# Another order of block products, background work tied behind weight splits, and two projections moved up in the third group

## The chip, the cores and the metric

The kernel runs on one core of a Trainium2 chip. The metric is the device time of one execution in microseconds (us). The kernel before took 1521.1 us, the median of three runs (1520.48 to 1521.79).

The engines of the core have these names in the profile: TensorE is PE (its weight loads are PEld), VectorE is DVE, ScalarE is ACT, GpSimd is POOL. SP issues most of the transfers (DMAs). Each engine has a queue of its own and runs it in order.

## The reference

Two layers of a mixer run on 256 tokens of width 2048, in float32, and a last RMS normalization follows:

```
u  = rms_norm(x, norm_g);  p = u @ w_in
qk, v, o, z_a, ig, fg, xb, z_b = split(p)
qk = silu(causal_dwconv(qk));  q, k = split(qk)
h  = mlstm_chunkwise(q, k, v, ig + i_bias, log_sigmoid(fg + f_bias))
h  = head_norm(h * sigmoid(o)) * head_norm_g;   y_a = h * silu(z_a)
xc = causal_dwconv(xb) + b
r, i = sigmoid(xc @ w_a + b_a), sigmoid(xc @ w_x + b_x)         # per head
log_a = -8 * r * softplus(-lam)
y_b = scan(h = a*h + xc*i*sqrt(1 - a^2)) * silu(z_b)
x  = x + concat(y_a, y_b) @ w_out
```

There are 8 mLSTM heads and 8 RG-LRU heads. The product with `w_in` (2048 by 12304) and the one with `w_out` (4096 by 2048) are most of the arithmetic.

## The kernel before

**Splits.** All products have to be as good as float32. TensorE's fast format keeps fewer bits, so each operand is split: a high part H (a cast on ScalarE, L344 of `prepare`, tile `wH`) and the low part L = value - H (a subtraction on VectorE, line L345, in the profile L189, the helper `tt_`; tile `wL`). A product is then three matmuls: H by H, H by L and L by H. The weights come from memory in units of 128 x 2048, which are worked off in two halves of 128 x 1024. `mm_a` makes 12 matmuls of 512 columns for each half.

**Order of the work.** `_sequence` lists the units of both layers. A layer has four groups of heads. A group consists of the projections o, qk, v, xb, z and zb (4 units, 8 halves each), the gate products (1 unit) and the output chunks of the group before (4 chunks of 2 units). The main loop (L1336) walks over the halves. At step n it first prepares the splits up to half n + 3 (`AHEAD = 3`; there are four buffers for H and four for L), then emits the matmuls of half n and what follows a finished accumulation (the `_post` functions, which evacuate PSUM).

**Background.** What follows a projection (convolutions, scores, the recurrence, the gate vector of the mLSTM) is written as generators in the queue `bg`. After each plain half, `pump` (L245) lets the generators run from the front until a budget is spent: 1.05 if at most two of them count, else 2.6. A generator yields the cost of what it has just emitted, or "wait" to be passed over, or None to end this turn of the pump. If something is needed now, `require` (L265) runs generators without a budget until it is there. The emitted program is then put into each engine's queue by a planner, which goes by its own estimate of when an instruction can run, and among those that can by the order of emission. `order(a, b)` (L237) makes the planner put a after b. It costs no instruction.

**Changes of layout.** `to_channels` turns a result from token order to channel order: ScalarE copies it to `tok`, VectorE transposes blocks of it to `blk`, four DMAs on SP's queue write it to memory as `moved`, and one DMA on Pool's queue reads it back as `fr`. q/k, xb and zb go through it, and so do z times the normalized heads, and x at the border of the layers. `joined` (L509) then copies `fr` to `ch` for the convolution.

**Block products.** The z projection of the third group and the o projection of the fourth (`PAIR`) have no place of their own in the order. Together they are a product of x, cut into 2 by 2 blocks (token half by half of the 2048 inputs), with weights cut into 2 by 2 blocks (input half by projection), and `block_halves` makes them in seven block products where eight would be the plain way. Products 5, 6, 7 and 3 need sums of blocks of x: `block_sums` makes S1 to S4 on VectorE (`sum_t`, `sums`) with a cast on ScalarE, in two buffers. Products 5, 6, 7 and 4 need sums of blocks of weights: `weight_sums` makes them in memory (`wd`, in the profile `w_d`) with DMAs, the first term as a copy on SP's queue, the others as accumulating DMAs on Pool's queue, one every four turns of the pump. Each product is four block halves of 6 matmuls; its result collects in one PSUM bank (`ps_b`) and is copied or added into one of four slots of `res`. The 28 block halves of a layer are spread evenly over a span of plain halves, except the eight halves that begin with a gate unit. The span of layer 0 begins with qk of the second group, that of layer 1 with v of the first (L1314); both end ahead of the third group's gates, where `z_post` takes the z result from `res`.

**The gate vector.** `first_gen` (L1146) of a layer makes the row scales, then `gates_gen` (tile `scs`: sums, a logarithm by a polynomial in `log1p_exp_half`, two scans), in layer 0 `lam_gen` (the same polynomial for lam, tile `lams`), then `gates_tr`, which puts the result at `at`, and it starts `block_sums`.

Of the kernel before, what the change touches and what calls it, by code (L numbers as in the profile page):

```python
# [16 lines left out]
P = 128  # L17
# [15 lines left out]
BLOCKS_AHEAD = 5  # L33

# [5 lines left out]
def _sequence():  # L40
# [54 lines left out]
def tile_trunk(ctx, tc, x, xt, par, gw, gb, ws, final_g, out):  # L95
    nc = tc.nc
    V, S, G, PE = nc.vector, nc.scalar, nc.gpsimd, nc.tensor
# [101 lines left out]
    def log1p_exp_half(x_, tl, behind=None):  # L199
# [5 lines left out]
        S.activation(out=z, in_=z, func=AF.Exp)  # L205
        d = tl("d")
        ts_(d, z, 2.0, ALU.add)
        V.reciprocal(out=d, in_=d)
        s = tl("s")
# [14 lines left out]
    def lam_gen():  # L224
        lams = work.tile([P, 4, DEPTH, 16], F32, tag="tok", name="lams")

        def tl_lam(nm):
            return lams[:, "zdsn".index(nm)]

        ql = log1p_exp_half(lam, tl_lam, st["split_end"])  # L230
# [314 lines left out]
    def gates_gen(l):  # L545
# [27 lines left out]
        G.memset(sT, 0.0)  # L573
        stt(sT[0:8, :], gi, gbs[:, l, 0:1], Fc, ALU.add, ALU.subtract)
# [10 lines left out]
        yield 3  # L585
# [231 lines left out]
    def gate_post(l, g):  # L817
        def gen():
            xc, _ = st["xc", l, g]
# [167 lines left out]
    def block_sums(l):  # L987
# [22 lines left out]
        def s2(two, a, k, ks):  # L1010
            order(stt(two[a], sums[0].bitcast(F32)[:, a, ks], -1.0, part(0, 0, a, k), ALU.mult, ALU.subtract), st["wL"])
# [4 lines left out]
        def s4(two, a, k, ks):  # L1016
            order(stt(two[a], sums[1].bitcast(F32)[:, a, ks], -1.0, part(0, 1, a, k), ALU.mult, ALU.subtract), st["wL"])
# [5 lines left out]
        while ("done", l, 5) not in st:  # L1023
            yield "wait"
        yield from made(0, "S3", s3)
        while ("done", l, 6) not in st:
# [8 lines left out]
    def weight_sums():  # L1035

        def moved(l, to, start, r, c):
            for j in range(2):
                for h in range(2):
                    cs = slice(1024 * h, 1024 * h + 1024)  # L1040
# [8 lines left out]
        for l in range(DEPTH):  # L1049
            yield from moved(l, 0, True, 0, 0)  # L1050
            yield from moved(l, 0, False, 0, 1)
            yield from moved(l, 1, True, 1, 1)
            yield from moved(l, 1, False, 0, 1)
            while ("loaded", l, 5) not in st:
                yield "wait"
            yield from moved(l, 0, False, 1, 1)
            while ("loaded", l, 6) not in st:
                yield "wait"
            yield from moved(l, 0, False, 1, 0)

    def block_halves(l):
# [19 lines left out]
        def end6():  # L1081
            add(1, 1, box["b"])
            add(3, 3, slot(1))

        def end7():
            add(2, 3, box["b"])
            add(1, 1, box["b"])

        def end4():
            add(1, 1, box["b"])  # L1090
            g1 = PAIR[1][1]

            def gen():
                while ("lru", l, g1 - 1) not in st:
                    yield "wait"
                o_post(l, g1, (slot(3), slot(2)), "neg")
# [22 lines left out]
        for no, A, need, end, W in (  # L1119
            (5, summed(0), "S1", lambda: copied(3), 0),  # L1120
            (1, plain(0, 0), None, lambda: copied(1), (0, 0)),
            (2, plain(0, 1), None, lambda: add(0, 1, box["b"]), (1, 0)),
            (6, summed(1), "S2", end6, 0),
            (7, summed(0), "S3", end7, 1),
            (3, summed(1), "S4", lambda: add(3, 3, box["b"]), (1, 1)),
            (4, plain(1, 1), None, end4, 0),
        ):
            for kp in range(4):
# [3 lines left out]
                if kp == 3:  # L1132
                    hf["loaded"] = ("loaded", l, no)
# [323 lines left out]
```

## Time and profile before

| | |
|---|---|
| median of three runs | 1521.1 us |
| the profiled execution | 1520.76 us |
| its span, first to last instruction | 1519.0 us |
| mean granted TensorE clock | 0.989 |
| PE busy | 1483.0 us, 98% |
| DVE busy | 1137.4 us, 75% |
| ACT busy | 969.9 us, 64% |
| POOL busy | 108.3 us, 7% |

Times inside a profile count from the start of the span. A busy share is the share of the span in which an engine had an instruction under way. The granted clock says at what part of its full speed TensorE was allowed to run. A row of groups has line, engine, operation, output<-inputs, shapes, count, then busy us, mean ns of one, and the idle time of the engine ahead of them with what ended it. A row of waits has the total, the number of waits and the longest.

### The profile page before, as it was taken

What the parts mean: (1) busy time and instruction counts of PE and PEld (TensorE: products, weight loads), DVE (VectorE), ACT (ScalarE), POOL (GpSimd) and SP (SyncE); (2) the same over time, 40 slices, a digit from 0 to 9 for tenths busy, and PEclk for the clock granted to TensorE, in tenths of its full rate; (3) what the DMA queues carried; (4) which work ended last, traced back from release to release, by engine and by line L of the source; (5) the groups of instructions that cost most, each with busy time, mean ns of one, the idle gap of its engine ahead of it and who ended that gap; (6) DMA issues with size and microseconds to landing.
All of it is one profiled execution on the core that took longest, in us unless ns stands there. A gap on an engine that the chain in (4) does not pass through costs nothing.

```text
span 1519.0 us, 18863 instructions
## 1 busy us (share of the span) xinstructions
PE 1483.0 (98%) x6782; PEld 1229.6 (81%) x6782; DVE 1137.4 (75%) x1616; ACT 969.9 (64%) x1259; POOL 108.3 (7%) x186
## 2 busy tenths in 40 slices
PE   9999999999999999999997899999999999999997
PEld 7878778888888878888885788888888888788886
DVE  5879977678757875778858897875886578766785
ACT  7656766567556775658664568754675567665675
POOL 0020011001000010000001100000000000000002
PEclk9999999999999999999999899999999999999999
DMA  9779798888889997876875696768976677678783
GB/s 348 277 244 280 277 281 246 274 276 276 284 264 311 281 269 251 251 258 218 286 269 153 195 279 230 256 203 257 282 260 233 218 239 224 213 243 267 238 277 111
DMA packets 104046, 383.44 MB, mean 252 GB/s; under 512 B 11392, under 2 KB 31888, under 8 KB 84496
## 3 DMA queue, kind: packets, MB, share of 16 engines
q1 hardware_dynamic: 87536, 327.41, 62.2%
q0 software_dynamic: 13952, 50.35, 15.2%
q10 hardware_dynamic: 2464, 4.47, 0.8%
q8 instruction: 53, 0.87, 0.2%
q14 instruction: 41, 0.34, 0.1%
HBM read 344.95 MB, written 62.41 MB: 268 GB/s over the span
## 4 chain that ended last, share of the span: by engine, by line
PE 85%; DVE 7%; DMA 4%; issue 3%; ACT 1%; POOL 0%; SPq 0%; DVEq 0%; POOLq 0%; ACTq 0%
PE acc L368 71%; PE ps_gt L807 3%; DVE wL L189 2%; PE ps_b L1108 2%; PE ps_b L1109 2%; PE ps_b L1107 2%; PE acc L381 1%; DMA raw<-in_ws_dram 1%; DMA moved<-blk 1%; DVE scs L189 1%; DMA w_d<-in_ws_dram 1%; PE acc L1202 1%; PE acc L1203 1%; PE acc L1201 1%; DMA fr<-moved 1%
## 5 line engine op out<-in xcount | busy, mean ns | idle before, releaser
L368 PE MATMUL acc<-wH,x_s 128*128 128x512 f32 x2752 | 865.4, 391 | 4.1 <-ACT wH L344 4.0
L189 DVE TENSOR_TENSOR wL<-raw,wH 128x1024 fp32r<-128x1024 f32 (+1 forms) x500 | 597.3, 1203 | 248.8 <-ACT wH L344 246.7
L344 ACT CAST wH<-raw 128x1024 fp32r<-128x1024 f32 (+1 forms) x500 | 513.9, 1037 | 339.3 <-PE acc L368 279.0
L368 PEld LDWEIGHTS acc<-wH,x_s 128*128 128x128 f32 x2752 | 519.4, 189 | 114.2 <-ACT wH L344 6.8
L368 PE MATMUL acc<-wL,x_s 128*128 128x512 f32 x1376 | 538.4, 392 | 21.1 <-DVE wL L189 21.1
L368 PEld LDWEIGHTS acc<-wL,x_s 128*128 128x128 f32 x1376 | 260.0, 189 | 78.2 <-DVE wL L189 24.9
L368 PE MATMUL acc<-wH,yaH 128*128 128x512 f32 x224 | 87.5, 390 | 0.0
L368 PE MATMUL acc<-wH,ybL 128*128 128x512 f32 x224 | 87.3, 390 | 0.0
L368 PE MATMUL acc<-wL,yaH 128*128 128x512 f32 x224 | 87.3, 390 | 0.0
L368 PE MATMUL acc<-wH,yaL 128*128 128x512 f32 x224 | 87.3, 390 | 0.0
L368 PE MATMUL acc<-wL,ybH 128*128 128x512 f32 x224 | 87.2, 389 | 0.0
L368 PE MATMUL acc<-wH,ybH 128*128 128x512 f32 x224 | 87.2, 389 | 0.0
L189 DVE TENSOR_TENSOR wL<-rawb,wH 128x1024 fp32r<-128x1024 f32 x56 | 68.4, 1222 | 23.7 <-ACT wH L344 21.5
L344 ACT CAST wH<-rawb 128x1024 fp32r<-128x1024 f32 x56 | 58.9, 1051 | 35.8 <-PE acc L368 25.8
L489 POOL DMA_DIRECT2D fr<-moved x34 | 19.3, 566 | 514.7 <-DMA moved<-blk 380.1
L485 DVE STREAM_TRANSPOSE blk<-tok 128x1024 f32<-128x1024 f32 x33 | 40.9, 1240 | 17.9 <-ACT tok L475 17.9
L368 PEld LDWEIGHTS acc<-wH,ybL 128*128 128x128 f32 x224 | 42.1, 188 | 9.0 <-DVE ybL L189 0.3
L368 PEld LDWEIGHTS acc<-wH,yaL 128*128 128x128 f32 x224 | 42.0, 188 | 8.7
L368 PEld LDWEIGHTS acc<-wL,ybH 128*128 128x128 f32 x224 | 42.0, 188 | 8.6
L368 PEld LDWEIGHTS acc<-wH,ybH 128*128 128x128 f32 x224 | 42.1, 188 | 8.6
L368 PEld LDWEIGHTS acc<-wH,yaH 128*128 128x128 f32 x224 | 42.1, 188 | 8.5
L368 PEld LDWEIGHTS acc<-wL,yaH 128*128 128x128 f32 x224 | 42.1, 188 | 8.2
(234 smaller groups left out, 1657.9 us busy)
## 6 DMA issues: line engine op xcount, KB each, us to landing
raw<-in_ws_dram SPq DMA_DIRECT2D x152, 1024.0 KB, 5.9
raw<-in_ws_dram SPq DMA_DIRECT2D x190, 512.0 KB, 6.2
fr<-moved POOLq DMA_DIRECT2D x34, 512.0 KB, 5.2
moved<-blk SPq DMA_DIRECT2D x132, 128.0 KB, 2.8
w_d<-in_ws_dram POOLq DMA_DIRECT2D x32, 512.0 KB, 12.8
rawb<-w_d SPq DMA_DIRECT2D x32, 512.0 KB, 6.8
rawb<-in_ws_dram SPq DMA_DIRECT2D x24, 512.0 KB, 5.4
x_d<-stage POOLq DMA_DIRECT2D x24, 512.0 KB, 7.2
```

Source lines behind the costliest of these rows:

```text
L189: return V.tensor_tensor(out=o, in0=a, in1=b, op=op)
L344: st["wH"] = S.copy(out=H[:, o], in_=r[:, o])
L368: st["mm"] = PE.matmul(o, a_[:, kt, P * t : P * t + P], W[:, k], start=b, stop=z)
L381: PE.matmul(ps[:, ct, T * part : 2 * T], W[:, k, P * ct : P * ct + P], moving, start=first and k == 0 and part == 0, stop=last and k == 3 ...
L485: V.transpose(out=blk.rearrange("p m n -> p (m n)"), in_=tok.rearrange("p m c t j -> p (m c t j)"))
L489: i0 = back.dma_start(out=fr.rearrange("p a c t i -> p a (c t i)"), in_=moved)
L807: PE.matmul(o, W[:, ib, jl], xs[:, ib, a, :], start=j == 0 and i == 0 and W is Hv and a == 0, stop=i == 1 and W is Lv, skip_group_check=True)
L1107: PE.matmul(box["b"], aH, Hv[:, k], start=kp == 0 and k == 0, stop=False)
L1108: PE.matmul(box["b"], aH, Lv[:, k], start=False, stop=False)
L1109: PE.matmul(box["b"], aL, Hv[:, k], start=False, stop=kp == 3 and k == 1)
L1201: PE.matmul(o, yH[:, kt, tsl], Hv[:, k, cs], start=start and k == 0, stop=False)
L1202: PE.matmul(o, yH[:, kt, tsl], Lv[:, k, cs], start=False, stop=False)
```

## The change

There are five parts.

1. **Order of the block products.** They come as 1, 2, 7, 5, 6, 3, 4; before it was 5, 1, 2, 6, 7, 3, 4. Products 1 and 2 take blocks of x as they are. The sums are made as S3, S1, S2, S4, and the first two when the first group's recurrence is done (`("lru", l, 0)`). The slots of `res` are used differently, with one copy more per layer, and some adds after product 6 become background. The sums of weights are made in the matching order, each accumulation allowed piece by piece.
2. **Span.** In layer 1 the block halves too begin with qk of the second group.
3. **Tie.** VectorE and ScalarE are wrapped, so that each instruction other than a split is ordered behind the last but one prepared split: behind its `wL` on VectorE, its `wH` on ScalarE.
4. **Third group.** Its order is qk, o, v, xb, four output chunks; before it was o, v, qk, two output chunks, xb, two output chunks.
5. **Yields.** The gate vector's generator yields small costs after few instructions; lam's part comes after `gates_tr`, has its tile elsewhere, and the recurrence waits for it (`"sp"`).

```diff
+LAG = 1
...
-            head = {0: ("o", "qk", "v"), 1: ("qk", "o", "v")}.get(g, ("o", "v", "qk"))
+            head = {0: ("o", "qk", "v"), 1: ("qk", "o", "v"), 2: ("qk", "o", "v")}.get(g, ("o", "v", "qk"))
             items = [("in", l, k, g) for k in head]
-            items += fill[0:2] + [("in", l, "xb", g)] + fill[2:4]
+            at = 0 if ("z", g) in PAIR else 2
+            items += fill[0:at] + [("in", l, "xb", g)] + fill[at:4]
...
+    done = {"wH": [], "wL": []}
+
+    class Behind:
+
+        def __init__(self, engine, key):
+            self.engine, self.key = engine, key
+
+        def __getattr__(self, name):
+            f = getattr(self.engine, name)
+
+            def g(*a, **k):
+                ins = f(*a, **k)
+                if st.get("behind"):
+                    order(ins, done[self.key][-1 - LAG])
+                return ins
+            return g
+
+    V, S = Behind(nc.vector, "wL"), Behind(nc.scalar, "wH")
...
         S.activation(out=z, in_=z, func=AF.Exp)
+        yield 0.25
...
         V.reciprocal(out=d, in_=d)
+        yield 0.8
...
         ts_(p, s2, 1.0 / 15, ALU.mult)
+        yield 0.5
         for c in (13, 11, 9, 7, 5, 3):
             stt(p, p, 1.0 / c, s2, ALU.add, ALU.mult)
+            if c % 4 == 1:
+                yield 0.4
         stt(p, p, 1.0, s, ALU.add, ALU.mult)
+        yield 0.25
...
-        lams = work.tile([P, 4, DEPTH, 16], F32, tag="tok", name="lams")
+        lams = act.tile([P, 4, DEPTH, 16], F32, tag="res", name="lams")
...
         for t_ in summed(x_, sc("z"), 32):
             tt_(x_, x_, t_, ALU.add)
+            yield 0.4
...
             tt_(gi, gi, t_, ALU.add)
-        yield 0.6
-        q = log1p_exp_half(x_, sc)
-        yield 4
+            yield 0.4
+        q = yield from log1p_exp_half(x_, sc)
...
         G.memset(sT, 0.0)
+        yield 0.6
...
         st["nG", l] = True
-        yield 3
+        yield 0.8
...
     def gate_post(l, g):
         def gen():
+            while "sp" not in st:
+                yield "wait"
...
-        while l == 0 and ("hn", 0, 0) not in st:
+        while ("lru", l, 0) not in st:
             yield "wait"
-        yield from made(0, "S1", s1)
-        yield from made(1, "S2", s2)
+        yield from made(0, "S3", s3)
+        yield from made(1, "S1", s1)
+        while ("done", l, 7) not in st:
+            yield "wait"
+        yield from made(0, "S2", s2)
         while ("done", l, 5) not in st:
             yield "wait"
-        yield from made(0, "S3", s3)
-        while ("done", l, 6) not in st:
-            yield "wait"
         yield from made(1, "S4", s4)
...
+            yield from moved(l, 1, True, 1, 1)
+            yield from moved(l, 1, False, 0, 1)
             yield from moved(l, 0, True, 0, 0)
             yield from moved(l, 0, False, 0, 1)
...
+            yield from moved(l, 0, False, 1, 1, 5)
+            yield from moved(l, 0, False, 1, 0, 6)
...
         def end6():
             add(1, 1, box["b"])
-            add(3, 3, slot(1))
-
-        def end7():
-            add(2, 3, box["b"])
-            add(1, 1, box["b"])
+
+            def gen():
+                add(2, 2, slot(1))
+                yield 1.2
+                add(1, 1, slot(3))
+                add(3, 3, slot(2))
+                yield 1.2
+            bg.append(gen())
...
-            (5, summed(0), "S1", lambda: copied(3), 0),
             (1, plain(0, 0), None, lambda: copied(1), (0, 0)),
             (2, plain(0, 1), None, lambda: add(0, 1, box["b"]), (1, 0)),
-            (6, summed(1), "S2", end6, 0),
-            (7, summed(0), "S3", end7, 1),
-            (3, summed(1), "S4", lambda: add(3, 3, box["b"]), (1, 1)),
+            (7, summed(0), "S3", lambda: copied(2), 1),
+            (5, summed(1), "S1", lambda: copied(3), 0),
+            (6, summed(0), "S2", end6, 0),
+            (3, summed(1), "S4", lambda: add(1, 1, box["b"]), (1, 1)),
             (4, plain(1, 1), None, end4, 0),
...
             yield from gates_gen(l)
+            yield from gates_tr(l)
             if l == 0:
                 yield from lam_gen()
-            yield from gates_tr(l)
+                st["sp"] = True
...
-        if (item[0], what) == ("in", ("v", 0) if l else ("qk", 1)) and l not in span:
+        if (item[0], what) == ("in", ("qk", 1)) and l not in span:
...
+            st["behind"] = False
             prepare(order_[nprep])
+            for key in done:
+                done[key].append(st[key])
+            st["behind"] = n >= 12
```

More of the change, by code (lines that the diff above doesn't have):

```diff
@@ L96, in tile_trunk @@
     nc = tc.nc
-    V, S, G, PE = nc.vector, nc.scalar, nc.gpsimd, nc.tensor
+    G, PE = nc.gpsimd, nc.tensor
+    done = {"wH": [], "wL": []}
[11 more added lines that the diff above has]
+    V, S = Behind(nc.vector, "wL"), Behind(nc.scalar, "wH")
     const = ctx.enter_context(tc.tile_pool(name="const", bufs=1))
@@ L1010, in s2 @@
         def s2(two, a, k, ks):
-            order(stt(two[a], sums[0].bitcast(F32)[:, a, ks], -1.0, part(0, 0, a, k), ALU.mult, ALU.subtract), st["wL"])
+            order(stt(two[a], sums[1].bitcast(F32)[:, a, ks], -1.0, part(0, 0, a, k), ALU.mult, ALU.subtract), st["wL"])
         def s3(two, a, k, ks):
@@ L1016, in s4 @@
         def s4(two, a, k, ks):
-            order(stt(two[a], sums[1].bitcast(F32)[:, a, ks], -1.0, part(0, 1, a, k), ALU.mult, ALU.subtract), st["wL"])
-        while l == 0 and ("hn", 0, 0) not in st:
-            yield "wait"
-        yield from made(0, "S1", s1)
-        yield from made(1, "S2", s2)
-        while ("done", l, 5) not in st:
+            order(stt(two[a], sums[0].bitcast(F32)[:, a, ks], -1.0, part(0, 1, a, k), ALU.mult, ALU.subtract), st["wL"])
+        while ("lru", l, 0) not in st:
             yield "wait"
         yield from made(0, "S3", s3)
-        while ("done", l, 6) not in st:
+        yield from made(1, "S1", s1)
+        while ("done", l, 7) not in st:
+            yield "wait"
+        yield from made(0, "S2", s2)
+        while ("done", l, 5) not in st:
             yield "wait"
@@ L1035, in weight_sums, with moved @@
     def weight_sums():
-        def moved(l, to, start, r, c):
+        def moved(l, to, start, r, c, no=None):
             for j in range(2):
                 for h in range(2):
+                    while no and ("loaded", l, no, 2 * j + h) not in st:
+                        yield "wait"
                     cs = slice(1024 * h, 1024 * h + 1024)
@@ L1095, in gen @@
                     yield "wait"
-                o_post(l, g1, (slot(3), slot(2)), "neg")
+                o_post(l, g1, (slot(1), slot(3)), "neg")
                 yield 0
@@ L1319, in tile_trunk @@
         b += b % 2
-        order_[b - 1]["then"] = lambda l=l: z_post(l, PAIR[0][1], st["res", l])
+        order_[b - 1]["then"] = lambda l=l: z_post(l, PAIR[0][1], st["res", l][:, 0:4:2])
         b -= 6
```

15 lines of the change are left out of this document (3 added, 12 removed).

## The prediction

> **What bounds the kernel now.** I read the page first: who is full, and how much idle time there is to win.
>
> ```profile
> span 1519.0 us, 18863 instructions
> PE 1483.0 (98%) x6782; PEld 1229.6 (81%) x6782; DVE 1137.4 (75%) x1616; ACT 969.9 (64%) x1259; POOL 108.3 (7%) x186
> ```
>
> TensorE is the bound. The change keeps its 6782 matmuls, so all it can win is idle time, 1519.0 - 1483.0 = 36.0 us, and time in which TensorE ran at a low clock. Next, the view of waits: what ends TensorE's idle time, and the longest wait of ScalarE.
>
> ```profile
> ACT wH L344 <- PE acc L368: 304.9, 229, 5.4
> ...
> PE acc L368 <- DVE wL L189: 21.1, 9, 14.8
> ```
>
> TensorE waits above all for the low half wL of a weight split, once for 14.8 us (columns: us in all, times, longest). Then the busy time by windows, cut at the places where TensorE was idle (window, length, busy time of PE, PEld, DVE, ACT, POOL; then granted clock, DMA share, GB/s):
>
> ```profile
> 51.00:93.00 42.00, 41.90 (x185) 34.36 (x183) 35.47 (x76) 22.01 (x28) 5.17 (x12) 1.00 0.73 235
> 93.00:98.00 5.00, 4.06 (x17) 3.22 (x18) 4.96 (x9) 3.33 (x4) 2.33 (x4) 1.00 0.07 16
> 135.00:170.00 35.00, 32.75 (x159) 27.16 (x158) 31.72 (x61) 25.88 (x42) 3.11 (x4) 0.95 0.83 256
> 170.00:218.00 48.00, 45.18 (x190) 36.35 (x189) 39.50 (x50) 33.70 (x40) 5.93 (x11) 0.96 0.88 286
> 518.00:543.00 25.00, 22.82 (x113) 18.53 (x112) 20.32 (x27) 21.64 (x34) 3.19 (x4) 0.93 0.94 258
> 811.00:825.00 14.00, 13.70 (x60) 10.71 (x58) 13.80 (x33) 9.33 (x13) 1.39 (x2) 1.00 0.84 194
> 825.00:841.00 16.00, 0.87 (x3) 0.44 (x3) 15.15 (x42) 6.09 (x9) 5.00 (x10) 0.60 0.05 17
> 841.00:847.00 6.00, 6.00 (x18) 4.73 (x19) 6.00 (x8) 3.73 (x6) 3.86 (x4) 0.64 0.73 261
> 847.00:1262.00 415.00, 415.00 (x1907) 346.10 (x1906) 311.27 (x415) 261.03 (x322) 19.05 (x35) 1.00 0.76 244
> 1262.00:1306.00 44.00, 41.56 (x204) 33.80 (x203) 39.29 (x70) 38.34 (x55) 2.45 (x5) 1.00 0.68 201
> ```
>
> The loss of a place is its idle time plus, where TensorE worked at a reduced clock, (1 - clock) times the length. 93-98: 0.9. 135-170 (first group's gates): 2.25 + 1.75 = 4.0. 170-218 (second group's q/k and the first block products): 2.8 + 1.9 = 4.7. 518-543 (third group's gates): 2.2 + 1.75 = 3.9. 811-847 (start of layer 1): 0.3 + 15.1 + 2.2 = 17.6. 1262-1306 (third group's gates again): 2.4. Together 33.5 us, over half of it in one place. The 26.2 us of idle time in these rows leave 9.8 of the 36.0 for the start, the last normalization and crumbs, which nothing here touches. From 847 to 1262 nothing is lost.
>
> **The large stall, step by step.** The timelines of TensorE, ScalarE and VectorE there (start, duration, instruction):
>
> ```profile
> 840.93 0.79 PE L368 MATMUL acc<-wL,x_s 128*128 128x512 f32 x1 [14.76 <-DVE wL L189]
> ```
> ```profile
> 819.89 1.03 ACT L344 CAST wH<-raw 128x1024 fp32r<-128x1024 f32 x1
> 820.82 1.05 ACT L344 CAST wH<-rawb 128x1024 fp32r<-128x1024 f32 x1
> ```
> ```profile
> 839.67 1.21 DVE L189 TENSOR_TENSOR wL<-raw,wH 128x1024 fp32r<-128x1024 f32 x1
> 840.80 1.21 DVE L189 TENSOR_TENSOR wL<-rawb,wH 128x1024 fp32r<-128x1024 f32 x1
> ```
>
> wH was there at 820.9, and its wL ran at 839.7: no data was late, the subtraction stood in VectorE's queue behind other work. What that work is, the groups of VectorE from 811 to 841 say (count, then busy us and mean ns):
>
> ```profile
> L192 DVE SCALAR_TENSOR_TENSOR scs<-scs 8x256 f32<-8x256 f32 x10 | 4.1, 406 | 0.0
> L189 DVE TENSOR_TENSOR sum_t<-x_s 128x256 f32<-128x256 f32 x8 | 3.2, 397 | 0.0
> L189 DVE TENSOR_TENSOR scs<-scs 8x256 f32<-8x256 f32 x6 | 2.4, 406 | 0.0
> L189 DVE TENSOR_TENSOR scs<-ps_g,rb 8x256 f32<-8x256 f32 x6 | 2.4, 414 | 0.1
> L189 DVE TENSOR_TENSOR sum_t<-sum_t 128x256 f32<-128x256 f32 x5 | 2.0, 407 | 0.0
> L208 DVE RECIPROCAL scs<-scs 8x256 f32<-8x256 f32 x1 | 1.7, 1734 | 0.0
> L189 DVE TENSOR_TENSOR sums<-sum_t,sums 128x256 fp32r<-128x256 f32 x4 | 1.6, 398 | 0.0
> ```
>
> The gate vector (scs) takes 4.1 + 2.4 + 2.4 + 1.7 = 10.6 us and the sums of x for the first block product 3.2 + 2.0 + 1.6 = 6.8. They came at once because that product requires S1 (L1115), and the requirement empties the whole background.
>
> **What the change does to it.** *Order of the products.* In layer 1 the block products now begin with q/k of the second group, as in layer 0, and products 1 and 2 need no sums. Nothing requires S1 at the layer's start, and S3 and S1 wait for the first group's recurrence. The 6.8 us leave this place for the stretch to 1262, where VectorE has 104 of 415 us free, and the 10.6 go back to the pump's pace. *The tie.* Each VectorE (ScalarE) instruction of the background and of the evacuations is ordered behind the wL (wH) of the last but one prepared half, n+2 at step n. The half that starved is n+1: between product 5's first part, which made the demand, and the stall TensorE issued only its wH products. So the tie reaches it. It adds no instruction and no wait between engines.
>
> What is left? The gates now cost the pump 6.0 units (four sums of 0.4, 3.0 in the logarithm, 0.6, 0.8) where they cost 7.6, and with three generators the pump spends 2.6 a half: 2.3 halves. How long a half is, the chain shows:
>
> ```profile
> 222.18 8.16 PE acc L368 x36
> ```
>
> 12 matmuls a half, so 8.16 / 3 = 2.72 us. VectorE gets 10.6 us of gates and 2.3 splits of 1.21 (2.8) in 2.3 x 2.72 = 6.3 us, 7.1 too many, against three halves split ahead (8.2). That is close, so I do not take zero. Below stands the first layer's start, the same gates, 0.9 lost; above, only the 6.8 us go: 17.6 - 6.8 = 10.8. I take 3.6, nearer the first row since it is the same work: **-14.0**.
>
> **First group's gates, 135-170.** The groups of VectorE there:
>
> ```profile
> L192 DVE SCALAR_TENSOR_TENSOR sum_t<-sums,x_s 128x256 f32<-128x256 f32 x8 | 3.4, 424 | 0.1
> L189 DVE TENSOR_TENSOR sums<-sum_t,sums 128x256 fp32r<-128x256 f32 x8 | 3.4, 420 | 0.2 <-ACT sums L1002 0.2
> L189 DVE TENSOR_TENSOR sum_t<-sum_t 128x256 f32<-128x256 f32 x8 | 3.3, 418 | 0.1
> L189 DVE TENSOR_TENSOR sum_t<-x_s 128x256 f32<-128x256 f32 x7 | 2.7, 416 | 0.0
> ```
>
> 12.8 us of sums leave this stretch of layer 0, since they now wait for its recurrence. VectorE falls from 31.7 to 18.9 of 35 us. Keep 0 to 4.0, taken 1.0: **-3.0**.
>
> **Second group's q/k, 170-218.** Here an instruction at the head of a queue is late (ScalarE, then VectorE):
>
> ```profile
> 207.98 1.05 ACT L511 COPY ch<-fr 128x1024 f32<-128x1024 f32 x1 [2.55 <-DMA fr<-moved]
> ```
> ```profile
> 210.05 2.46 DVE L192 SCALAR_TENSOR_TENSOR qc<-ch,pars,qc 128x255 f32<-128x255 f32 x6 [5.71 <-ACT qc L457]
> ```
>
> The channel copy waits for its DMA and the convolution for the copy, with splits behind both. The tie does not bring the DMA sooner, but puts one or two more splits ahead of it. Keep 0 to 4.7, taken 2.2: **-2.5**. Product 1 has its matrix straight from the weights.
>
> **Third group's gates.** ScalarE, from evacuating xb to its cast for the gates:
>
> ```profile
> 1247.11 1.27 ACT L475 ACTIVATE tok<-acc,rstd 128x512 f32<-128x512 f32 x2 [1.67 <-PE acc L368]
> ...
> 1280.05 0.62 ACT L787 CAST xcs<-xc 128x512 fp32r<-128x512 f32 x1 [1.16 <-DVE xc L192]
> ```
>
> 33 us, while the program leaves 8 plain halves (two output chunks) between xb and gates: 22 us, and some blocks. So gates are reached before xc and force the rest. After the change four chunks stand there, 16 halves or 44 us, as in the second group, whose gates lie in the lossless stretch to 1262. q/k moves from third to first place, so the head normalization that z's evacuation requires is earlier too. With q/k and xb move their transposing DMAs on SP's queue (four each) and the return on Pool's (one each), ahead of the accumulating DMAs of two output chunks; those sums are read only in the last group, so nobody waits for them. Keep 0 to 3.9 and 0 to 2.4, taken 1.0 and 0.6: **-2.9 and -1.8**.
>
> **Small parts.** At 93-98 lambda's polynomial now follows the gates and no longer delays them; **-0.4** of 0.9. The recurrence, which now waits for it, comes only with the gates in 135-170. One copy into res more per layer:
>
> ```profile
> L1079 ACT COPY res<-ps_b x4: 562/583/590, 222.8 to 956.7; 128x512 f32<-128x512 f32 x4
> ```
>
> 0.6 us, covered by ScalarE's free 154 of 415 us; uncovered it would be 1.2 in all. The weight sums keep their 48 DMAs. Product 6 now follows 5 directly, and its accumulated weights must land in between: four parts and some 14 halves, 40 us, against
>
> ```profile
> w_d<-in_ws_dram POOLq DMA_DIRECT2D x32, 512.0 KB, 12.8
> ```
>
> so nothing. S3 and S1 arrive in 183-218, in front of the second group's convolution: **+1.0** (0 to 4.0, what 12.8 us of sums cost in 135-170).
>
> **Sum.** -14.0 - 3.0 - 2.5 - 2.9 - 1.8 - 0.4 + 1.0 = -23.6. The profiled execution took 1520.8, 0.3 under the median: 1497.2, and 1497.5 as a median, so 1497.
>
> The Trainium skill (TensorE: Matmul & The Clock Gate, "Why this matters for your kernels") warns of idle gaps over some 3 us, after which the clock falls. By it the short gaps before 543 would cost idle time alone, 5.4 us of clock would not be there to win, and the sum would be nearer 1501. The trace disagrees: 135-170 has 2.25 us of idle in all and a clock of 0.95.
>
> **Rivals.** *All of it goes* (0.17): only the 0.9 us that the first layer's gates cost stays, 33.5 - 0.9 = 32.6 off: 1488. For it: the lossless 415 us. Against: late DMAs stay.
>
> *The gates alone still swamp VectorE* (0.15): layer 1 keeps 10.8, the others gain as much as they lose, +1.0: 1521.1 - 6.8 + 1.0 = 1515. For it: 7.1 us too many. Against: 51-93, VectorE 84% busy, 0.1 lost.
>
> *The planner's queues do not follow* (0.04): the splits stood early enough and were late for another cause: 1521. Against: the 18.8 us between wH and wL.
>
> *The tie slows the background* (0.09): wH waits 304.9 us for TensorE to free buffers, and now everything on ScalarE behind it waits too. If the 33 us from xb to xcs grow past the 44 us that the program leaves, by 11 us over some eight hops, all eight gates force their background at 4.0 each: 32 + 3.6 + 4.7 = 40.3 against 33.5, so 1528. Against: a half is split ahead, so each hop waits less than a half. The same skill page ("Architectural detail") has ScalarE and VectorE as strict first-in-first-out, which is what this rival needs; 207.98 above agrees.
>
> **How the numbers follow.** Forecast 0.55, with its own range 1491 to 1508. 1486 to 1516 takes in the first two rivals and the bounds; outside lie the tie, the idle planner and edges, under 0.2. This kernel tells 0.2% (3 us) from no change: faster 0.87, same 0.05, slower 0.08.
>
> **What would show it.** Right: no wait over 4 us on wL near 811-847, sums after the first recurrence in both layers, full clock at the third gates. Wrong: a new wait of TensorE on wH or xcs at several gates, VectorE waiting for wL with work behind it, or scs still ahead of a wL whose wH is done.

## The result and the profile after

The changed kernel takes 1499.3 us (median of four runs, 1494.89 to 1501.92); the kernel before, beside it, 1520.79 (1520.45 to 1521.79). The ratio is 0.9855, 95% interval 0.9831 to 0.9879: 21.5 us faster. The forecast was 1497.

The profiled execution is the fastest of the four, 1494.89 us. Its page, top and TensorE's share, shows the same 6782 matmuls:

```profile
span 1493.2 us, 18858 instructions
PE 1475.0 (99%) x6782; PEld 1226.1 (82%) x6782; DVE 1145.7 (77%) x1616; ACT 967.0 (65%) x1258; POOL 104.4 (7%) x186
```

Of 36.0 us of idle time, 18.2 are left, and TensorE's busy time fell by 8.0, about the 7.6 us of reduced clock in the prediction's rows. VectorE and ScalarE have the same work as before: nothing was saved, things were moved. The windows of the changed kernel, cut at the places of the prediction (window, length, busy time of PE, PEld, DVE, ACT, POOL; granted clock, DMA share, GB/s):

```profile
93.00:98.00 5.00, 5.00 (x24) 4.14 (x23) 4.96 (x9) 2.02 (x3) 1.41 (x4) 1.00 0.31 102
135.00:170.00 35.00, 33.04 (x168) 27.78 (x167) 27.15 (x32) 24.42 (x36) 1.44 (x2) 1.00 0.80 231
170.00:218.00 48.00, 46.83 (x207) 38.47 (x206) 42.86 (x67) 34.97 (x46) 4.43 (x9) 1.00 0.86 298
500.00:540.00 40.00, 40.00 (x202) 33.97 (x201) 32.07 (x34) 34.29 (x48) 4.29 (x6) 1.00 0.90 286
740.00:770.00 30.00, 28.45 (x123) 22.68 (x122) 17.90 (x16) 22.44 (x38) 3.46 (x6) 1.00 0.95 325
800.00:850.00 50.00, 48.59 (x214) 39.67 (x213) 39.90 (x68) 26.30 (x31) 5.19 (x16) 1.00 0.54 178
1225.00:1290.00 65.00, 65.00 (x312) 54.76 (x311) 51.61 (x58) 49.97 (x66) 4.33 (x7) 1.00 0.81 239
```

The third group's gates lose nothing in either layer (500-540, 1225-1290). The start of layer 1 (800-850) lost 17.6 us and now 1.4, and a further 0.95 just behind 850. The first group's gates keep 2.0, the second group's q/k 1.2. A loss that was not there before stands at the border of the layers, 740-770: 1.6.

What VectorE does at the start of layer 1 now (its timeline):

```profile
811.30 1.21 DVE L111 TENSOR_TENSOR wL<-raw,wH 128x1024 fp32r<-128x1024 f32 x1
812.43 1.73 DVE L111 RECIPROCAL scs<-scs 8x256 f32<-8x256 f32 x1
814.10 1.15 DVE L111 TENSOR_TENSOR wL<-raw,wH 128x1024 fp32r<-128x1024 f32 x1
```

The gate vector is still here, but from 808 us on a split comes after every one to five of its steps, and no sum of x is near. That is the picture the prediction asked for. What is left of TensorE's waits in the changed kernel (engine, who it waits for, us in all, times, longest):

```profile
PE acc L394 <- DVE wL L111: 4.0, 6, 1.2
PE acc L394 <- ACT wH L111: 1.7, 2, 1.4
PE ps_gt L834 <- ACT gate L111: 1.6, 1, 1.6
```

The longest wait for wL went from 14.8 us to 1.2. The third row is new: TensorE waits for a PSUM bank that ScalarE has not yet evacuated.

### The profile page after: what moved, and what is told of

It is laid out like the page before. It is cut to its first block, busy times and chain, and to the rows that moved or that the text cites. A ratio compares the mean times of both kernels' runs of the same rounds, so it can differ in the third digit from the quotient of the medians.

```text
span 1493.2 us, 18858 instructions
## 1 busy us (share of the span) xinstructions
PE 1475.0 (99%) x6782; PEld 1226.1 (82%) x6782; DVE 1145.7 (77%) x1616; ACT 967.0 (65%) x1258; POOL 104.4 (7%) x186
## 4 chain that ended last, share of the span: by engine, by line
PE 78%; DMA 5%; ACT 4%; DVE 3%; issue 3%; SPq 0%; ACTq 0%; POOL 0%; DVEq 0%; POOLq 0%
PE acc L394 65%; PE ps_gt L834 2%; DMA raw<-in_ws_dram 2%; PE ps_b L1137 2%; PE ps_b L1138 2%; PE ps_b L1139 2%; DMA x_d<-stage 1%; DVE wL L111 1%; PE acc L407 1%; DMA fr<-moved 1%; ACT wH L111 1%; ACT gate L111 1%; PE acc L1232 1%; PE acc L1231 1%; PE acc L1233 1%
## 5 line engine op out<-in xcount | busy, mean ns | idle before, releaser
L111 DVE TENSOR_TENSOR wL<-rawb,wH 128x1024 fp32r<-128x1024 f32 x56 | 68.3, 1220 | 15.7 <-ACT wH L111 14.7
L111 DVE STREAM_TRANSPOSE blk<-tok 128x1024 f32<-128x1024 f32 x33 | 41.0, 1241 | 11.3 <-ACT tok L111 10.8
```

The lines of the kernel that those rows point to most:

```text
L111: ins = f(*a, **k)
```

## The experiments

Each kernel is compared with the kernel before on the same chip. That kernel's median was 1522.5 in the first four comparisons, 1521.4 in the next four and 1522.6 in the last four; differences in us are against these.

**The tie left out.** The changed kernel with

```diff
-            st["behind"] = n >= 12
+            st["behind"] = False
```

> The changed kernel without the tie (everything else stays). If the order of the products and the span cure the stall at the start of layer 1, and the tie only helps in small places, this takes 1501 to 1506 us, 3 to 7 over the changed kernel, and no single wait of TensorE on wL is over 5 us. If the tie is what cures the stall, the gate vector's 10.6 us still stand ahead of a wL there: a wait of 6 to 10 us near 800 to 850 and 1508 to 1515 us in all.

Measured: 1491.4 us (1491.1 to 1493.1), ratio 0.9798 (0.9784 to 0.9813). It is *faster* without the tie, by some 8 us. Windows of this kernel: behind the wait shown next, over the first two groups' gates and q/k together, at the border and at the start of layer 1:

```profile
97.60:104.40 6.80, 6.76 (x19) 5.37 (x20) 6.74 (x9) 6.24 (x7) 2.23 (x4) 0.63 0.46 154
135.00:218.00 83.00, 82.95 (x390) 69.29 (x389) 73.83 (x109) 62.28 (x85) 9.06 (x14) 1.00 0.87 281
740.00:770.00 30.00, 30.00 (x134) 24.86 (x133) 20.06 (x24) 25.63 (x46) 2.90 (x5) 1.00 0.95 325
795.00:850.00 55.00, 55.00 (x245) 45.28 (x244) 45.69 (x74) 31.08 (x37) 6.12 (x17) 1.00 0.67 209
```

With everything but the tie, nothing is lost at the start of layer 1 or at the border, and 0.05 us from 135 to 218. One loss appears instead, 4.05 us and then (1 - 0.63) x 6.8 = 2.5 of clock; TensorE's and VectorE's timelines of this kernel:

```profile
97.64 0.80 PE L394 MATMUL acc<-wL,x_s 128*128 128x512 f32 x1 [4.05 <-DVE wL L111]
```
```profile
95.44 1.01 DVE L111 TENSOR_SCALAR E<-nb,at 128x256 f32<-128x256 f32 x4 [7.83 <-DMA nb<-nG_d]
```

The first scores (E) wait 7.8 us at the head of VectorE for their broadcast to come back by DMA, and the next split follows at 96.36. The tie removes this one: the window 93-98 of the changed kernel is full.

**The tie alone.** The kernel before with LAG, the class Behind, the two lines that make V and S from it, the lists in done, and the flag:

```diff
+    V, S = Behind(nc.vector, "wL"), Behind(nc.scalar, "wH")
...
+            st["behind"] = n >= 12
```

> The kernel before with the tie alone. If the demand for S1 is the cause, the tie can only put the halves already prepared (up to three, 8.2 us of matmuls) ahead of the burst, so about half of the 17.6 us at the start of layer 1 stays: 1508 to 1513 us. If the tie alone is the cure, the stall is under 4 us and the time 1498 to 1503 us. If the tie holds up the background, the gates lose more and the time is 1521 us or above.

Measured: 1530.6 us (1528.9 to 1533.8), ratio 1.0056 (1.0040 to 1.0071): 8.0 us slower. The stall at the start of layer 1 is where it was (TensorE, then VectorE's last split before the gap and the first behind it):

```profile
847.90 0.79 PE L387 MATMUL acc<-wL,x_s 128*128 128x512 f32 x1 [14.71 <-DVE wL L110]
```
```profile
824.08 1.21 DVE L110 TENSOR_TENSOR wL<-raw,wH 128x1024 fp32r<-128x1024 f32 x1
...
846.64 1.21 DVE L110 TENSOR_TENSOR wL<-raw,wH 128x1024 fp32r<-128x1024 f32 x1
```

Between the two splits stand the same gates, sums and convolution as before. The half that starves is not one that was prepared when S1 was demanded: its split was issued after the demand, so nothing could be tied behind it. In the kernel before, VectorE's four plain splits between the split of product 5's first part and that of its second (803.72 and 840.80) show it:

```profile
803.72 1.23 DVE L189 TENSOR_TENSOR wL<-rawb,wH 128x1024 fp32r<-128x1024 f32 x1 [0.16 <-ACT wH L344]
810.18 1.23 DVE L189 TENSOR_TENSOR wL<-raw,wH 128x1024 fp32r<-128x1024 f32 x1 [5.24 <-ACT wH L344]
815.96 1.23 DVE L189 TENSOR_TENSOR wL<-raw,wH 128x1024 fp32r<-128x1024 f32 x1
817.43 1.21 DVE L189 TENSOR_TENSOR wL<-raw,wH 128x1024 fp32r<-128x1024 f32 x1
839.67 1.21 DVE L189 TENSOR_TENSOR wL<-raw,wH 128x1024 fp32r<-128x1024 f32 x1
```

Counted from the block part they are n+1 to n+4, and the starved one is n+4. The tie reaches n+2.

**The place of the block products alone.** The kernel before, layer 1's products beginning with q/k of the second group as in layer 0, in their old order:

```diff
-        if (item[0], what) == ("in", ("v", 0) if l else ("qk", 1)) and l not in span:
+        if (item[0], what) == ("in", ("qk", 1)) and l not in span:
```

> The kernel before with one line changed: in layer 1 the block halves begin with q/k of the second group (products still in the order 5, 1, 2, 6, 7, 3, 4, no tie). If the demand for S1 at the start of layer 1 is the cause, the 14.8 us wait goes and with it 10 to 15 us: 1506 to 1511 us. If the gate vector alone swamps VectorE, a wait of over 6 us on wL stays near 825 and the time is 1512 to 1518 us.

Measured: 1515.1 us (1512.4 to 1515.9), ratio 0.9949 (0.9932 to 0.9966): 7.4 us. The stall is gone whole, but only half of it is won. Windows of this kernel at the start of layer 1 and at the first group's gates of layer 1, where the kernel before lost nothing:

```profile
805.00:845.00 40.00, 40.00 (x179) 32.80 (x178) 34.27 (x62) 20.86 (x26) 2.32 (x5) 1.00 0.61 190
890.00:925.00 35.00, 30.90 (x150) 25.32 (x149) 29.44 (x59) 26.40 (x41) 0.64 (x2) 0.95 0.42 134
```

4.1 us idle and (1 - 0.95) x 35 = 1.75 of clock. The sums, made early, stand just ahead of this window and not in it: VectorE spends 8.5 us on them between 850 and 890, where it is busy 38.0 of 40 us, and 1.2 us between 890 and 925. TensorE's longest wait in the window is for the gates' input xcs, 1.4 us. That the sums make xcs late is a reading, not shown. The rest of what is not won lies at the third groups' gates: 500-545 loses 7.4 us (before 4.0) and 1225-1306 3.8 (before 2.4). Why was not looked into.

**The old products with the rest of the change.** The changed kernel with sums, weight sums, products and their place as before:

```diff
-        while ("lru", l, 0) not in st:
+        while l == 0 and ("hn", 0, 0) not in st:
...
+            (5, summed(0), "S1", lambda: copied(3), 0),
             (1, plain(0, 0), None, lambda: copied(1), (0, 0)),
             (2, plain(0, 1), None, lambda: add(0, 1, box["b"]), (1, 0)),
-            (7, summed(0), "S3", lambda: copied(2), 1),
-            (5, summed(1), "S1", lambda: copied(3), 0),
...
-        if (item[0], what) == ("in", ("qk", 1)) and l not in span:
+        if (item[0], what) == ("in", ("v", 0) if l else ("qk", 1)) and l not in span:
```

> The changed kernel with the old order of products, the old sums and the old span (tie, third group and yields stay). If the order of products carries most of the gain, 1507 to 1512 us, with a wait of 6 us or more at the start of layer 1 and losses at 135 to 218 as before. If the tie carries it, 1499 to 1503 us.

Measured: 1517.3 us (1515.5 to 1519.6), ratio 0.9969 (0.9957 to 0.9980). The longest wait for wL is 14.7 us again, though the gates have their new yields and the tie is on: neither helps this stall.

**The old third group, no tie.**

```diff
-            head = {0: ("o", "qk", "v"), 1: ("qk", "o", "v"), 2: ("qk", "o", "v")}.get(g, ("o", "v", "qk"))
+            head = {0: ("o", "qk", "v"), 1: ("qk", "o", "v")}.get(g, ("o", "v", "qk"))
...
-            at = 0 if ("z", g) in PAIR else 2
+            at = 2
...
-            st["behind"] = n >= 12
+            st["behind"] = False
```

> The changed kernel without the tie (1491.4 us) and with the third group in the old order. If the moved q/k and xb are what freed the third group's gates in both layers (3.9 and 2.4 us before), these losses come back near 520 and 1260: 1496 to 1499 us. If the other parts had freed them, 1490 to 1493 us.

Measured: 1499.4 us (1496.5 to 1502.0), ratio 0.9855 (0.9838 to 0.9872), against 0.9798 with the new third group. So the third group's order is worth 0.0057 x 1521 = 8.7 us, with some 3 us of uncertainty from the two intervals. The losses at its gates are back (windows of this kernel):

```profile
505.00:536.00 31.00, 28.82 (x139) 23.41 (x138) 26.28 (x40) 25.84 (x39) 1.41 (x2) 0.94 0.80 262
1245.00:1275.00 30.00, 27.81 (x142) 22.81 (x141) 25.28 (x37) 25.01 (x39) 1.40 (x2) 1.00 0.63 198
```

2.2 + (1 - 0.94) x 31 = 4.1, and 2.2: together 6.3 of the difference.

**The old yields, no tie.** The logarithm of the gates again in one piece, with yields of 0.6, 4 and 3 around it:

```diff
...
-        q = yield from log1p_exp_half(x_, sc)
+        yield 0.6
+        q = log1p_exp_half(x_, sc)
+        yield 4
...
-        yield 0.8
+        yield 3
...
```

> The changed kernel without the tie and with the old yields of the gate vector (lam's part still after the gates). If the pump's pace for the gate vector decides nothing once no sums are demanded beside it, 1490 to 1493 us. If the fine yields keep the start of layer 1 free, a wait on wL near 800 to 830 comes back and the time is 1494 to 1500 us.

Measured: 1490.7 us (1488.0 to 1492.4), ratio 0.9796 (0.9781 to 0.9811), beside 0.9798 with the new yields. The finer yields are worth nothing that can be told, at least without the tie. The new place of lam's part stayed and was not tested by itself.

**The first scores later, no tie.** To see whether the 4.05 us at 97 can be had without the tie, E of the first group comes eight turns of the pump later, and behind the newest split:

```diff
+        for _ in range(8 if g == 0 else 0):
+            yield "wait"
...
+            if g == 0:
+                order(i0, st["wL"])
```

> The changed kernel without the tie, and the first group's E (the decay matrix) emitted eight turns of the pump later, which puts its VectorE instructions behind at least one more split. Without the tie TensorE lost 6.6 us at 97 to 103, where E waited 7.8 us for its DMA at the head of VectorE's queue. If that wait is the cause, 3 to 6 us go: 1485 to 1488.5 us. If the loss only moves to the scores, which need E, 1490 to 1493 us.

Measured: 1492.1 us (1488.6 to 1492.3), ratio 0.9802 (0.9787 to 0.9816). No gain: the loss moved to the scores. TensorE's longest wait is now for the scores' own sums (dn), 2.3 us.

**The tie one half looser.** LAG = 2, behind the last but two:

```diff
-LAG = 1
+LAG = 2
```

> The changed kernel with the tie one half looser (behind the last but two prepared split). If the tie costs because the background stands behind a split that itself waits, for its weights' DMA or for a buffer that TensorE frees, a split one half older is done sooner and most of the 8 us go: 1491 to 1495 us. If any tie costs, because it changes the planner's order, 1497 to 1501 us.

Measured: 1492.7 us (1491.7 to 1495.1), ratio 0.9816 (0.9800 to 0.9833). Most of what the tie costs is gone. That fits the first reading: a background instruction that stands behind a waiting split is released sooner. This kernel loses nothing at the scores, at the first gates or from 740 to 890; 1.1 us stay in 170-218 and 2.5 us at 413-418.

**The changed kernel again.** So that the 8 us are not one chip against another, it ran once more beside the last three kernels, without an edit.

> The changed kernel itself, on the chip of the three that follow. If the 8 us between it and the kernel without the tie are the tie's and not another chip's, it stays at 1496 to 1502 us. If they were the chip's, 1490 to 1493 us.

Measured: 1498.6 us (1494.7 to 1500.5), ratio 0.9845 (0.9827 to 0.9863). The cost of the tie stands.

**The tie only at the start.** Steps 12 to 45, where it has the scores' wait to remove:

```diff
-            st["behind"] = n >= 12
+            st["behind"] = 12 <= n < 46
```

> The changed kernel with the tie only in the first group of layer 0 (steps 12 to 45). There it puts E, which waits for a DMA, behind more splits (the kernel without the tie lost 6.6 us at 97 to 103, the changed one 0.4), and it is absent where it delayed evacuations. If both readings hold: 1484 to 1488 us, faster than either. If the tie's cost sits in the first group, 1492 to 1498 us.

Measured: 1488.2 us (1484.6 to 1489.3), ratio 0.9776 (0.9759 to 0.9793): the fastest kernel of this study, 34.4 us under the kernel before and 10.5 under the changed one beside it. The longest wait that is left of TensorE (its waits for wL are 1.4 us in all), and the window of the first scores, which is full:

```profile
PE ps_gt L834 <- ACT gate L111: 1.5, 1, 1.5
```
```profile
93.00:103.00 10.00, 10.00 (x45) 8.28 (x45) 8.61 (x10) 7.13 (x8) 0.00 (x0) 1.00 0.47 143
```

Against the kernel without a tie it removes 6.6 us at 97 but is only 3.2 us faster. The wait for the gate's bank, which it shares with the changed kernel and the one without a tie does not have, says where some of it went. In the changed kernel (TensorE's first gate, ScalarE's cast and evacuation, TensorE's wait):

```profile
146.33 0.40 PE L834 MATMUL ps_gt<-xcs,wH 128*128 128x256 f32 x2
...
152.58 0.50 PE L834 MATMUL ps_gt<-xcs,wH 128*128 128x256 f32 x2 [1.65 <-ACT gate L111]
```
```profile
147.22 1.05 ACT L111 CAST wH<-raw 128x1024 fp32r<-128x1024 f32 x1 [5.02 <-DMA raw<-in_ws_dram]
...
151.69 1.57 ACT L111 ACTIVATE gate<-ps_gt,pars 128x256 f32<-128x256 f32 x4
```

And in the kernel without a tie:

```profile
152.86 0.40 PE L834 MATMUL ps_gt<-xcs,wH 128*128 128x256 f32 x2
```
```profile
151.57 1.05 ACT L111 CAST wH<-raw 128x1024 fp32r<-128x1024 f32 x1 [2.85 <-DMA raw<-in_ws_dram]
```

In the kernel with the tie and in the one without, the cast stands at the head of ScalarE waiting for its weights. Without the tie the stall at 97 has put TensorE 6.5 us later, and the weights are there 1.3 us before the first gate; with it, 0.9 us after, and the evacuations queue behind. The transfers did not come 6.5 us sooner because TensorE did, but 4.35. So the wait stands where the stall at 97 is gone, and part of what the stall cost returns here. It need not: with LAG = 2 TensorE begins these gates at 145.91, ScalarE's cast gets its weights at 143.97, and nothing is lost. Why the weights come sooner there was not followed.

**The tie on one engine.** First VectorE alone, then ScalarE alone:

```diff
-    V, S = Behind(nc.vector, "wL"), Behind(nc.scalar, "wH")
+    V, S = Behind(nc.vector, "wL"), nc.scalar
```

> The changed kernel with VectorE's instructions tied and ScalarE's not. ScalarE makes the evacuations and its splits wait for buffers and weights (wH behind TensorE 289 us, behind a weights' DMA up to 5.0 us). If the cost of the tie is there, this takes 1486 to 1492 us. If it is VectorE's, 1496 to 1502 us.

```diff
-    V, S = Behind(nc.vector, "wL"), Behind(nc.scalar, "wH")
+    V, S = nc.vector, Behind(nc.scalar, "wH")
```

> The changed kernel with ScalarE's instructions tied and VectorE's not: the counterpart. If the cost of the tie is ScalarE's, 1496 to 1502 us, with a wait of TensorE on the gates' sigmoid near 152. If it is VectorE's, 1488 to 1493 us.

Measured: VectorE's tie 1491.4 us (1490.3 to 1492.4), ratio 0.9801 (0.9787 to 0.9815), which is the kernel without a tie; ScalarE's 1499.2 (1495.9 to 1501.8), ratio 0.9851 (0.9833 to 0.9869), which is the changed kernel. The whole difference between the changed kernel and the one without a tie hangs on ScalarE's tie. VectorE's comes out even, which is not the same as free: the scores' 6.6 us are gone and the time stays, since this kernel loses 2.2 us in 545-740, 1.1 in 135-170 and less elsewhere. Against the tie at the start only it is 3.3 us slower, with intervals that overlap (that kernel's windows at the scores and at the start of layer 1, then TensorE's waits in the one with ScalarE's):

```profile
93.00:103.00 10.00, 10.00 (x46) 8.28 (x45) 9.94 (x14) 7.31 (x9) 0.77 (x2) 1.00 0.86 284
...
800.00:860.00 60.00, 60.00 (x269) 49.77 (x268) 49.04 (x76) 33.56 (x39) 6.90 (x17) 1.00 0.65 219
```
```profile
PE acc L394 <- DVE wL L209: 8.0, 9, 2.6
PE acc L394 <- ACT wH L111: 2.1, 2, 1.7
```

Where the tie costs: beside the kernel with the tie at the start only, the changed kernel loses 1.2 us more in 170-218, 1.6 at the border and 2.4 at the start of layer 1, 5.2 of the 7.8 us between the two profiled spans (1493.2 and 1485.4). The border is not ScalarE's tie alone: the kernel that has only that one loses nothing in 740-770. The times at which TensorE begins the gates agree: from the fourth group's of layer 0 to the first group's of layer 1 it takes 216.1 us in the changed kernel (673.90 to 889.97), 210.4 with the tie at the start only (671.75 to 882.19) and 210.1 without a tie (676.02 to 886.15).

The other two places can be read from the one-engine kernels. First the start of layer 1, ScalarE's timeline with its tie on:

```profile
826.91 1.05 ACT L111 CAST wH<-raw 128x1024 fp32r<-128x1024 f32 x1 [1.66 <-PE acc L394]
827.87 1.04 ACT L111 COPY ch<-fr 128x1024 f32<-128x1024 f32 x1
...
841.73 1.04 ACT L111 CAST wH<-raw 128x1024 fp32r<-128x1024 f32 x1
846.26 1.28 ACT L111 ACT_TABLE_LOAD   x1 [3.49 <-DVE qc L212]
...
849.66 1.99 ACT L111 CAST wH<-raw 128x1024 fp32r<-128x1024 f32 x2
```

and with only VectorE's:

```profile
806.53 1.05 ACT L537 COPY ch<-fr 128x1024 f32<-128x1024 f32 x1 [0.96 <-DMA fr<-moved]
...
845.14 2.00 ACT L370 CAST wH<-raw 128x1024 fp32r<-128x1024 f32 x2
```

The channel copy ch of the second group's q/k runs 21.3 us later with ScalarE's tie, though fr is there at about 807 in both (issued at 803.12, landed 3.9 us later); eight casts go ahead of it. At the same step of layer 0 the copies are at 212.9 and 198.6. So the convolution behind it starts late and is not done when ScalarE reaches its sigmoid: ScalarE stands 3.49 us at the table load, no cast comes from 842.8 to 849.7, and TensorE waits 1.74 + 0.96 us for wH and wL. With VectorE's tie alone 800-860 loses nothing. Why the copy falls back by eight casts and not by two is open. One reading is that the planner, left free, places it ahead of the work it was issued with, and the tie forbids that; this was not tested.

Then 170-218, where the kernel with ScalarE's tie loses 2.6 us idle and 1.9 of clock. Its timelines of ScalarE, VectorE and TensorE:

```profile
172.22 1.05 ACT L111 CAST wH<-raw 128x1024 fp32r<-128x1024 f32 x1 [5.06 <-DMA raw<-in_ws_dram]
173.18 1.70 ACT L111 ACTIVATE tok<-fr,pars 128x256 f32<-128x256 f32 x4
...
176.00 1.23 DVE L209 TENSOR_TENSOR yaL<-tok,yaH 128x1024 fp32r<-128x1024 f32 x1 [3.13 <-ACT yaH L111]
...
178.99 0.53 PE L394 MATMUL acc<-wL,x_s 128*128 128x512 f32 x1 [2.59 <-DVE wL L209]
```

A cast waits 5.06 us for its weights with the background's tok behind it; VectorE waits 3.13 us for what follows from tok, with the next split behind that; and TensorE waits for that split. In the three kernels whose ScalarE is free here (no tie, the tie at the start only, VectorE's alone) the same tok goes ahead of that cast, with VectorE's tie at 169.31 and the cast at 172.30, and none of them loses time at 178. In the changed kernel the order is that of the tied one, the cast waits 3.62 us for a buffer, and TensorE loses 1.2. So here the tie's price is background held behind a split that itself waits. The border was not read to its end.

## Why the prediction was right, and where it was not

The total, 1497 against 1499.3, is right. That it fits so closely is luck: one term has the wrong sign and others are too small, and these errors nearly cancel. By the prediction's own places (idle time plus lost clock in us: before, predicted to stay, changed kernel, changed kernel without the tie):

| Place | Before | Kept, predicted | Changed | No tie |
|---|---|---|---|---|
| 93-98 (no tie: to 104), scores | 0.9 | 0.5 | 0 | 6.6 |
| 135-170, first gates | 4.0 | 1.0 | 2.0 | 0 |
| 170-218, second q/k | 4.7 | 3.2 with S3 and S1 | 1.2 | 0 |
| third gates | 3.9 | 1.0 | 0 | 0 |
| start of layer 1 | 17.6 | 3.6 | 2.4 | 0 |
| third gates again | 2.4 | 0.6 | 0 | 0 |
| border of the layers | 0 | 0 | 1.6 | 0 |

Changed column: 33.5 - 7.2 = 26.3 us off, and the profiled executions differ by 1520.8 - 1494.9 = 25.9. So the places account for that execution; its three sisters are 4 to 7 us slower. The repeat, profiled at 1499.0, shows where its 4.1 us lie: much the same waits, but with a clock that fell behind the one at the gates and behind the one at 852 (last section). For the kernel without a tie the places fall short: 33.5 - 6.6 = 26.9, where the profiled executions differ by 29.7. So they place only 0.6 of the 3.8 us between its span and the changed kernel's. A wait of 0.7 us at 630 in the changed kernel is another part; the rest was not placed.

**Large stall, order of the products: right, and stronger than said.** The step "nothing requires S1 at the layer's start" carried it. The bounds ran from 0.9 to 10.8; without the tie the loss is 0, below both. The estimate counted 13.4 us of VectorE work against 6.3 us of pump time and took the 7.1 too many as near the 8.2 of halves split ahead; VectorE met it without a loss. The kernel with the place alone shows that the place removes the stall, and that the new order of the products and sums is what keeps the win: without it 5.9 us come back at layer 1's first gates, and the kernels that have it lose 0.3 there without the tie, with the old third group or the old yields too.

**Large stall, the tie: wrong.** The failed step is "The half that starved is n+1 ... So the tie reaches it". It is n+4, issued after the demand; the tie alone leaves 14.7 of the 14.8 us. The rows that say so (the four splits between the two block splits) were in the trace of before.

**The tie elsewhere: the wrong sign.** It stood in the sum as a help (part of the -2.5 at 170-218) and costs 8 us: 8.0 on the kernel before, 7 to 9 on the changed one (0.9845 to 0.9855 against 0.9798 to 0.9801). The only place where it is seen to help the changed kernel is the first scores (0.9 us before, 6.6 without it); the prediction named lambda's polynomial there, not the tie. The rival "the tie slows the background", with 0.09, had the sign, the engine and the mechanism: background on ScalarE comes later. It had the wrong place and price: it let xc come late and force eight gates, 40.3 us, and no wait of TensorE on xcs is there in the changed kernel. With the tie alone on the kernel before there are two, 2.9 us together, so the rival's path exists, at a small part of its price. What comes late in the changed kernel is the copy of q/k's channels and the evacuation at 173, and their price is a wait or two in a layer.

**First gates: right in cause, under-sized.** With the sums gone VectorE is busy 27.2 of 35 us, not 18.9, since other work moved in; without the tie nothing is lost. The 2.0 kept are what the earlier arrival at the gates finds in this kernel, weights that are not there yet, and not sums.

**Second group's q/k.** The tie was to put "one or two more splits ahead" of the late copy and win 2.5. It puts the copy itself 14 us later, and the place loses 1.2 with the tie and nothing without; that 1.2 falls at 177.8, ahead of the copy, where an evacuation stands behind a waiting cast.

**S3 and S1 at 183-218, +1.0: not seen.** The sums do land there, and without the tie 135-218 loses 0.05 us in all.

**Third group: under-sized.** -4.7 predicted, 6.3 of 6.3 gone from the profile and 8.7 in the times. The reason, four output chunks between xb and gates, stands: putting the old order back brings the losses back at the same two gates. Nothing was seen of SP's and Pool's queues.

**Yields: no part.** The prediction gave the gates a finer pace with weight in the 14.0; without the tie, taking them out again changes nothing. Beside the tie they were not tested.

**What would show it.** "No wait over 4 us on wL near 811-847" and full clock at the third gates held. Of the signs against, no wait on wH or xcs came at the gates. What came, a wait for the gates' banks and late splits at the border and at 849, was not on the list.

**Rivals.** "All of it goes", 1488, is what the best variant reaches (1488.2), with the tie taken back to where it helps; the changed kernel does not reach it. "The gates alone swamp VectorE" and "the planner's queues do not follow" fell.

Effects are not additive: the tie (+8.0) and the third group (-8.7) would leave the old products where the kernel before is, and they are 5.3 us faster (that kernel has the new yields too).

## What to carry to other kernels

Work that an order written by hand demands at one point empties everything behind it: move the demand away from a place where the same engine is already full, and then see where the moved work lands, since the move alone gave back half. The same ordering rule came out even on one engine and cost 8 us on another. At the two places that were read it held back an instruction that a later chain hung on. Try such a rule engine by engine and place by place, and keep it only where a row shows the wait that it removes. A stall removed early lets TensorE arrive sooner at transfers that need not come as much sooner, so part of it can return downstream.

## What the runs showed of the hardware

The clock can fall after a gap of some 1.5 to 2.5 us, and need not. At the first gates the changed kernel's two profiles have the same wait. In the repeat it is longer by 0.45 us, and the clock is reduced behind it (TensorE, then the window after the wait; after that the same window of the first profile):

```profile
153.35 0.50 PE L834 MATMUL ps_gt<-xcs,wH 128*128 128x256 f32 x2 [2.10 <-ACT gate L111]
153.00:158.00 5.00, 4.65 (x19) 4.17 (x20) 4.97 (x6) 4.89 (x10) 0.00 (x0) 0.66 0.56 199
```
```profile
152.60:156.00 3.40, 3.40 (x21) 3.07 (x22) 3.37 (x5) 3.38 (x8) 0.00 (x0) 1.00 0.54 140
```

The length of the gap alone does not decide. In the kernel before, a gap of 1.49 us that ended at 165.19 was followed by a mean clock of 0.66 over 5 us; in the kernel with the old third group one of 2.58 us that ended at 95.55 was followed by 1.00. The Trainium skill (TensorE: Matmul & The Clock Gate, "Why this matters for your kernels") puts the rule at idle gaps over some 3 us. Gaps of 3.10, 3.93, 4.05 and 14.76 us in four of the kernels agree, each followed by a clock of 0.50 to 0.66; the shorter gaps that were followed by 0.66 disagree.

These drops make up most of the difference between the changed kernel's two profiled executions (spans 1493.2 and 1497.3). The first has a clock of 1.00 in both windows; the repeat has 0.95 in 135-170 and 0.96 in 850-890, (1 - 0.95) x 35 + (1 - 0.96) x 40 = 3.4 of the 4.1 us. For the other runs of this kernel, 1494.7 to 1501.9 us with granted clocks from 0.995 to 0.998, the same is likely and was not shown.
